# Two-layer decoder trunk on one core: smaller adding transfers in the MLP, and a later row scale in layer 1

## The chip, the cores and the metric

The kernel runs on one core of a Trainium2 chip. The metric is device time in microseconds. Three runs of the kernel before took 605.1, 606.25 and 607.38 us, a median of 606.25. The engines named below are TensorE (PE; PEld is its weight load), VectorE (DVE), ScalarE (ACT), GpSimd (POOL) and SyncE (SP), each with a queue of its own that is worked off in order.

## The reference

The input is one sequence of 256 rows with 1024 channels in 32-bit floats. Two layers follow each other, then a last RMSNorm.

```
h = x
for i in range(2):
    hn = rmsnorm(h, attn_norm[i])
    m  = diff_attention(hn, ...) if i == 0 else moba_attention(hn, ...)
    h  = h + m
    h  = h + square(relu(rmsnorm(h, mlp_norm[i]) @ w_ff1[i])) @ w_ff2[i]     # 1024 -> 4096 -> 1024
out = rmsnorm(h, final_norm)
```

Layer 0's mixer has 8 heads, each with two softmaxes whose difference weighs the values. Layer 1's has 16 heads of 64 channels with block choice, which at 256 rows and blocks of 256 comes to plain causal attention. Both project with one matrix w_in to q, k and v and then with w_out. Per layer that is 12 MB of w_in, 4 MB of w_out and 16 MB each of w_ff1 and w_ff2, all read from HBM.

## The kernel before, in words

**Splitting.** TensorE multiplies in a rounded form of 32-bit floats. To keep the accuracy, every operand is split into a high part (the rounded value) and a low part (what rounding left). A product is then three matmuls: high by high, high by low, low by high. All weights pass through this split on the chip.

**Blocks of weights.** Weights come in blocks of 1 MB (128 partitions x 2048 values). `load` (L148) issues a block's transfer on SP's queue into one of four `raw` buffers; the split writes `hi` and `lo` buffers, of which there are five each. A block's transfer waits until the split four blocks earlier has released its `raw` buffer; a split waits until TensorE has released a `hi` and `lo` buffer. `need` (L220) asks, wherever a matmul uses a block, for loads up to six blocks ahead and for splits up to three ahead.

**Three ways of splitting.** In the plain way (`split_part`, L194), ScalarE copies raw to the rounded high part (L195) and VectorE subtracts it from raw to get the low part (L196), in pieces of 1024 values, or in one piece of 2048 where a unit's `how` is the number RING (2048). The blocks of w_ff2 (`split_sums`, L165) also form sums and differences of their four quarters (L177, L179, L180), since the second product is done with seven matmuls in place of eight; their last step is a piece of 2048 (high by ScalarE, low by VectorE). The blocks of w_ff1 from column group j = 1 on are split "partly" (`split_partly`, L184). A block there has KC = 8 row groups of 256 values per partition. The first OWN = 3 groups are split in the plain way, in a piece of 768. For the other five, ScalarE writes the high part (L189) and then its negative into `lo` (L190), and a transfer that GpSimd issues (L191) reads the same weights from HBM a second time and adds them to `lo`.

```
k = slice(OWN, KC)
nc.scalar.activation(hi[:, k], raw[:, k], AF.Copy)
nc.scalar.activation(lo[:, k], hi[:, k].bitcast(F32), AF.Copy, scale=-1.0)
nc.gpsimd.dma_start(lo[:, k], units[u]["pieces"][0][1][:, k], accum_op=ALU.add)
split_part(raw[:, :OWN], hi[:, :OWN], lo[:, :OWN])
```

**The MLP.** `mlp` works through pairs of 256 hidden columns p = 0 to 15; blocks (j, a) of w_ff1 and w_ff2 belong to p = 2j + a. `f1` (L692) multiplies by a w_ff1 block: for each 128 columns it goes through the row groups kc = 0 to 7 with three matmuls each (L702, L703, L704; L704 uses `lo`). `hidden` (L708) makes the squared ReLU on ScalarE (L715, L716), its sums on VectorE (L720 to L722) and its split (gh, gl). `f2` (L730, matmuls at L744) multiplies by a w_ff2 block, two pairs behind; the products of pairs 13 and 14 come last (`product`), then pair 15 (`direct`, L754).

**The order.** Within the MLP and at the head of layer 1, no order is written out: a planner orders each engine's instructions from the program's order, the dependences and its own estimates of duration, with splits set back in priority (LATER). In the rest of the mixers TensorE's order is the program's. Layer 0's head has its whole order written out.

**The head of layer 1.** The mixer's first matmuls use the transposed, not yet scaled rows `xT`. The factor of each row, one over the root mean square, is computed by GpSimd (`root_r`, L326), spread over the partitions by two transposes on TensorE (`scale_r`, L384) and copied to `R` by ScalarE (L385, L386). `qk` (L388) accumulates q and k of a head pair into one bank `z` (L396 to L398), and `qk_out` (L402) multiplies `z` by `R` on VectorE (L405). In layer 1 the order of calls is: row groups 0 to 3 of head 0's q and k, the first half of v, `root_r`, `scale_r`, row groups 4 to 7 of head 0's q and k, the second half of v (L581 to L586).

Of the kernel before, what the change touches and what calls it, by code (L numbers as in the profile page):

```python
# [24 lines left out]
RING = 2048  # L25
# [2 lines left out]
WARM = 12  # L28
LATER = 150
SOONER = 100  # L30
OWN = 3


@with_exitstack
def kernel(
# [33 lines left out]
    def ptile(*a, **k):  # L69
        return phase["pool"].tile(*a, **k)  # L70
# [19 lines left out]
    units = []  # L90
# [6 lines left out]
    for i in range(2):  # L97
# [27 lines left out]
        def f1_unit(j, a):  # L125
            c = j * 512 + a * 256
            U[i, "f1", j, a] = unit([P, KC, 256], [((slice(None),), f1[:, :, c:c + 256])])
            if j:
                units[-1]["how"] = "partly"

        def f2_unit(j, a):
            U[i, "f2", j, a] = unit([P, 2, D], [
# [240 lines left out]
    def mixer(i, parts):  # L373
# [3 lines left out]
        def root_r():  # L377
            S["r"] = rsqrt(f"a{i}", mean_eps(f"a{i}", parts))

        def scale_r():  # L380
            r = S["r"]
            t_ps = ps("tp", f"rps{i}")
            for t in range(NT):
                nc.tensor.transpose(t_ps[:, t * P:(t + 1) * P], r[:, t:t + 1].to_broadcast([P, P]), ident)  # L384
            nc.scalar.activation(R[:, :T], t_ps[:, :T], AF.Copy, scale=-HD ** -0.5)  # L385
            nc.scalar.activation(R[:, T:], t_ps[:, :T], AF.Copy)  # L386
# [15 lines left out]
        def qk_out(h):  # L402
            o = ptile([P, 2 * T], F32, tag="qk", name=f"qk{i}_{h}", bufs=4)
            with tc.high_priority(offset=SOONER):
                nc.vector.tensor_tensor(o, S["z", h], R, op=ALU.mult)  # L405
            S["qk", h] = o[:, :T], o[:, T:]
# [155 lines left out]
        if i == 0:  # L562
            with tc.manual_schedule():
                parts = start()
                root_r()
                xt = xT[i, "a"]
                qk(0, 0, 0, 8, out=False)
                qk(0, 1, 0, 8, out=False)
                v(0, 0)
                split_until(3)  # L570
                lambda_sums()
                scale_r()
                qk_out(0)
                split_until(5)
                v(0, 1)
                lambda_out()
                load_gains()
            state["ahead"] = LOOK
        else:
            xt = xT[i, "a"]  # L580
            qk(0, 0, 0, 4); qk(0, 1, 0, 4)  # L581
            v(0, 0)
            root_r()
            scale_r()
            qk(0, 0, 4, 8); qk(0, 1, 4, 8)
            v(0, 1)  # L586


# [362 lines left out]
```

## Time and profile before

| What | Value |
|---|---|
| median of three runs | 606.25 us (605.1 to 607.38) |
| the profiled execution | 607.94 us, of which the span of instructions is 606.2 |
| TensorE busy | 577.5 us (95%) |
| VectorE busy | 460.8 us (76%) |
| ScalarE busy | 411.4 us (68%) |
| GpSimd busy | 104.1 us (17%) |
| bytes moved | 122.28 MB, of them 18.37 MB on GpSimd's queue |
| mean granted TensorE clock | 0.98 |

How to read it: all times are from one execution. "Busy" counts an engine's instructions, and "idle before" is the time an engine stood still ahead of an instruction, with the instruction that released it behind "<-". `lo<-in_w_ff_dram` on GpSimd's queue is the adding transfer; `raw<-in_w_ff_dram` on SP's is the plain load. Buffer numbers are left out of names. The granted clock is TensorE's share of full speed. A group's line gives its count, then busy time and mean ns of one instruction behind the first bar, and idle time behind the second.

### The profile page before, as it was taken

What the parts mean: (1) busy time and instruction counts of PE and PEld (TensorE: products, weight loads), DVE (VectorE), ACT (ScalarE), POOL (GpSimd) and SP (SyncE); (2) the same over time, 40 slices, a digit from 0 to 9 for tenths busy, and PEclk for the clock granted to TensorE, in tenths of its full rate; (3) what the DMA queues carried; (4) which work ended last, traced back from release to release, by engine and by line L of the source; (5) the groups of instructions that cost most, each with busy time, mean ns of one, the idle gap of its engine ahead of it and who ended that gap; (6) DMA issues with size and microseconds to landing.
All of it is one profiled execution on the core that took longest, in us unless ns stands there. A gap on an engine that the chain in (4) does not pass through costs nothing.

```text
span 606.2 us, 9768 instructions
## 1 busy us (share of the span) xinstructions
PE 577.5 (95%) x3784; PEld 516.0 (85%) x3784; DVE 460.8 (76%) x740; ACT 411.4 (68%) x640; POOL 104.1 (17%) x109
## 2 busy tenths in 40 slices
PE   7999998999899999997979999999999999999985
PEld 6899897799799898986769988878988999898964
DVE  3898487299889898977784664645997989888774
ACT  6876466388878778767464555646887787787543
POOL 6011001101110101100050760601011010110003
PEclk9999999999999999999899999999998999999978
DMA  9996633159999999974687535433699999999501
GB/s 299 288 318 209 189 103 128 68 115 270 263 286 231 271 255 252 317 178 127 199 244 203 179 140 148 139 131 50 169 265 279 249 272 222 275 250 273 148 0 69
DMA packets 103486, 122.28 MB, mean 202 GB/s; under 512 B 2544, under 2 KB 86288, under 8 KB 103440
## 3 DMA queue, kind: packets, MB, share of 16 engines
q1 hardware_dynamic: 84752, 103.03, 53.6%
q0 software_dynamic: 18528, 18.37, 20.0%
q8 instruction: 29, 0.48, 0.3%
q10 hardware_dynamic: 160, 0.27, 0.1%
q14 instruction: 17, 0.14, 0.1%
HBM read 120.60 MB, written 1.05 MB: 201 GB/s over the span
## 4 chain that ended last, share of the span: by engine, by line
PE 38%; DVE 24%; issue 14%; ACT 11%; DMA 9%; POOL 2%; SPq 0%; POOLq 0%; DVEq 0%; ACTq 0%
DVE lo L196 7%; DVE tlo L196 5%; PE z L396 5%; PE z L397 4%; PE m L744 4%; PE z L398 4%; DMA lo<-in_w_ff_dram 4%; DMA raw<-in_w_ff_dram 3%; DVE gl L196 3%; ACT hi L195 2%; DVE raw L180 2%; PE wo L552 2%; PE v L419 2%; PE v L417 2%; PE v L418 2%
## 5 line engine op out<-in xcount | busy, mean ns | idle before, releaser
L195 ACT ACTIVATE hi<-raw 128x1024 fp32r<-128x1024 f32 (+3 forms) x136 | 158.7, 1186 | 89.8 <-DVE raw L180 40.7
L196 DVE TENSOR_TENSOR lo<-raw,hi 128x1024 fp32r<-128x1024 f32 (+3 forms) x134 | 184.2, 1396 | 38.3 <-ACT hi L195 37.0
L191 POOL DMA_DIRECT2D lo<-in_w_ff_dram x28 | 42.2, 1508 | 285.6 <-ACT lo L190 224.5
L704 PE MATMUL f<-xT_(1, 'm')_4429,lo 128*128 128x256 f32 x256 | 72.3, 283 | 2.3 <-DMA lo<-in_w_ff_dram 2.3
L704 PE MATMUL f<-xT_(0, 'm')_1447,lo 128*128 128x256 f32 x256 | 71.4, 279 | 2.6 <-DMA lo<-in_w_ff_dram 2.6
L703 PE MATMUL f<-xT_(1, 'm')_4429,hi 128*128 128x256 f32 x256 | 72.1, 282 | 0.0
L702 PE MATMUL f<-xT_(1, 'm')_4429,hi 128*128 128x256 f32 x256 | 72.0, 282 | 0.0
L702 PE MATMUL f<-xT_(0, 'm')_1447,hi 128*128 128x256 f32 x256 | 71.5, 280 | 0.0
L703 PE MATMUL f<-xT_(0, 'm')_1447,hi 128*128 128x256 f32 x256 | 71.4, 280 | 0.0
L744 PE MATMUL m<-hi,gh 128*128 128x512 f32 x120 | 47.8, 401 | 4.6 <-ACT hi L195 4.6
L704 PEld LDWEIGHTS f<-xT_(1, 'm')_4429,lo 128*128 128x128 f32 x256 | 48.5, 190 | 2.7 <-DMA lo<-in_w_ff_dram 2.7
L744 PE MATMUL m<-lo,gh 128*128 128x512 f32 x120 | 49.0, 408 | 1.8 <-DVE lo L196 1.8
L704 PEld LDWEIGHTS f<-xT_(0, 'm')_1447,lo 128*128 128x128 f32 x256 | 47.9, 187 | 2.8 <-DMA lo<-in_w_ff_dram 2.8
L702 PEld LDWEIGHTS f<-xT_(1, 'm')_4429,hi 128*128 128x128 f32 x256 | 48.7, 191 | 0.7
L703 PEld LDWEIGHTS f<-xT_(1, 'm')_4429,hi 128*128 128x128 f32 x256 | 48.7, 190 | 0.6
L702 PEld LDWEIGHTS f<-xT_(0, 'm')_1447,hi 128*128 128x128 f32 x256 | 48.0, 188 | 0.9 <-ACT g L715 0.3
L703 PEld LDWEIGHTS f<-xT_(0, 'm')_1447,hi 128*128 128x128 f32 x256 | 48.0, 188 | 0.6
L744 PE MATMUL m<-hi,gl 128*128 128x512 f32 x120 | 48.4, 403 | 0.0
L195 ACT ACTIVATE gh<-g 128x1024 fp32r<-128x1024 f32 (+1 forms) x32 | 33.0, 1031 | 20.9 <-DVE g L722 20.6
L196 DVE TENSOR_TENSOR gl<-g,gh 128x1024 fp32r<-128x1024 f32 (+1 forms) x32 | 38.0, 1187 | 10.8 <-ACT gh L195 10.8
L189 ACT ACTIVATE hi<-raw 128x1280 fp32r<-128x1280 f32 x28 | 35.3, 1259 | 13.4 <-PE wo L554 13.4
L177 DVE TENSOR_TENSOR ts<-raw 128x1024 f32<-128x1024 f32 x30 | 36.5, 1218 | 6.4 <-DMA raw<-in_w_ff_dram 6.4
(232 smaller groups left out, 1475.4 us busy)
## 6 DMA issues: line engine op xcount, KB each, us to landing
raw<-in_w_ff_dram SPq DMA_DIRECT2D x64, 1024.0 KB, 6.6
lo<-in_w_ff_dram POOLq DMA_DIRECT2D x28, 640.0 KB, 10.2
raw<-in_w_in_dram SPq DMA_DIRECT2D x30, 512.0 KB, 6.8
raw<-in_w_in_dram SPq DMA_DIRECT2D x8, 1024.0 KB, 6.3
raw<-in_w_out_dram SPq DMA_DIRECT2D x8, 1024.0 KB, 5.1
xs<-in_x_dram SPq DMA_DIRECT2D x2, 512.0 KB, 3.8
raw<-in_w_in_dram SPq DMA_DIRECT2D x4, 256.0 KB, 7.0
fg<-in_final_norm_dram SPq DMA_DIRECT2D x1, 512.0 KB, 7.0
```

The costliest lines, as they stand in the source:

```text
L177: tt(ts, r4[:, 1:2].to_broadcast([P, 2, h]), r4[:, 0:4:3], op=sub)
L189: nc.scalar.activation(hi[:, k], raw[:, k], AF.Copy)
L191: nc.gpsimd.dma_start(lo[:, k], units[u]["pieces"][0][1][:, k], accum_op=ALU.add)
L195: nc.scalar.activation(h, r, AF.Copy)
L196: eng.tensor_tensor(l, r, h.bitcast(F32), op=ALU.subtract)
L396: mm(z, hi[:, s, kc], xh, start=s == 0 and kc == 0, stop=False, skip_group_check=True)
L397: mm(z, hi[:, s, kc], xl, start=False, stop=False, skip_group_check=True)
L398: mm(z, lo[:, s, kc], xh, start=False, stop=s == 1 and kc == KC - 1, skip_group_check=True)
L702: mm(z, hi[:, kc, c], xh, start=f % 2 == 0 and kc == 0, stop=False, skip_group_check=True)
L703: mm(z, hi[:, kc, c], xl, start=False, stop=False, skip_group_check=True)
L704: mm(z, lo[:, kc, c], xh, start=False, stop=f % 2 == 1 and kc == KC - 1, skip_group_check=True)
L744: mm(M[k], x[:, g], y, start=p == 0 and x is gh and y is hi, stop=p == LAST - 1 and x is gl, skip_group_check=True)
```

## The change

OWN becomes 5, so five of a partly split block's eight row groups are split in the plain way and the adding transfer covers three. The two blocks with j = 1 of each layer are no longer split partly but in the plain way, in one piece of 2048; they have no adding transfer. In layer 1, `scale_r` is called after row groups 4 to 7 of head 0's q and k, and `qk_out` for head 0 after it.

```diff
-OWN = 3
+OWN = 5
@@ f1_unit
             if j:
-                units[-1]["how"] = "partly"
+                units[-1]["how"] = "partly" if j > 1 else RING
@@ mixer, layer 1
             v(0, 0)
             root_r()
+            qk(0, 0, 4, 8); qk(0, 1, 4, 8, out=False)
             scale_r()
-            qk(0, 0, 4, 8); qk(0, 1, 4, 8)
+            qk_out(0)
             v(0, 1)
```

## The prediction

> **What bounds the kernel now.** First the page and the waits of TensorE (columns: us in total, times, longest). TensorE is busy 95% of the span, so only its stalls and its clock can be won.
>
> ```profile
> span 606.2 us, 9768 instructions
> PE 577.5 (95%) x3784; PEld 516.0 (85%) x3784; DVE 460.8 (76%) x740; ACT 411.4 (68%) x640; POOL 104.1 (17%) x109
> ...
> PE f L704 <- DMA lo<-in_w_ff_dram: 4.9, 2, 2.6
> PE m L744 <- ACT hi L195: 4.6, 2, 2.9
> PE rps L384 <- POOL rs_a L326: 3.3, 1, 3.3
> ...
> PE m L744 <- DVE lo L196: 1.8, 2, 0.9
> ```
>
> The change touches all four. The first sits early in each MLP: a matmul wants low parts that an adding transfer has not delivered. The second and fourth sit at the end of each MLP, on the split of the last block but one of w_ff2. The third sits at the head of layer 1.
>
> Then the busy time by stage (length, PE, PEld, DVE, ACT, POOL, granted clock, DMA share, GB/s). The first two rows are the MLPs of layers 0 and 1, from their first matmul to the end of that last split.
>
> ```profile
> 122.00:285.60 163.60, 157.30 (x1059) 143.71 (x1057) 142.77 (x176) 127.28 (x143) 19.70 (x14) 1.00 0.92 237
> 419.00:582.70 163.70, 158.91 (x1058) 145.31 (x1056) 142.74 (x175) 127.15 (x141) 19.54 (x13) 0.99 0.89 227
> ...
> 285.00:292.00 7.00, 6.31 (x15) 4.96 (x16) 7.00 (x8) 5.91 (x9) 0.00 (x0) 0.51 0.75 231
> ...
> 316.20:319.60 3.40, 3.36 (x18) 3.37 (x19) 0.00 (x0) 1.60 (x3) 0.00 (x0) 0.57 1.01 377
> ...
> 455.60:459.10 3.50, 3.14 (x14) 3.15 (x15) 2.91 (x4) 3.43 (x3) 0.00 (x0) 0.51 0.92 305
> ```
>
> The reader is to see three things. TensorE idles 6.3 us in the first MLP (163.60 less 157.30), VectorE 20.8. Behind a stall the granted clock falls to about half. And the two MLPs are equally long to 0.1 us although layer 1 has a stretch at half clock after its early stall (455.60) that layer 0 has not, some 1.7 us of TensorE time. What TensorE loses early in an MLP is therefore not seen at its end: the end is set by the chain of splits on VectorE and ScalarE. This decides how I cost the change.
>
> VectorE's own waits in layer 0's MLP, and its last turns:
>
> ```profile
> DVE gl L196 <- ACT gh L195: 5.4, 6, 1.2
> DVE g L720 <- ACT g L716: 4.6, 6, 1.0
> DVE lo L196 <- ACT hi L195: 4.3, 3, 2.0
> DVE ts L177 <- DMA raw<-in_w_ff_dram: 4.1, 2, 2.7
> ...
> 261.52 1.23 DVE L177 TENSOR_TENSOR ts<-raw 128x1024 f32<-128x1024 f32 x1 [2.73 <-DMA raw<-in_w_ff_dram]
> ...
> 273.34 2.29 DVE L196 TENSOR_TENSOR lo<-raw,hi 128x2048 fp32r<-128x2048 f32 x1 [1.98 <-ACT hi L195]
> ...
> 277.81 1.22 DVE L196 TENSOR_TENSOR gl<-g,gh 128x1024 fp32r<-128x1024 f32 x1 [1.19 <-ACT gh L195]
> ...
> 283.35 4.49 DVE L196 TENSOR_TENSOR lo<-raw,hi 128x2048 fp32r<-128x2048 f32 x2 [1.98 <-ACT hi L195]
> ```
>
> The three last turns (1.98, 1.19, 1.98: 5.2 us) are VectorE handing to ScalarE and waiting for the answer. They stay. The other waits on ScalarE (14.3 less 5.2: 9.1) and on transfers (4.1) are what can give way.
>
> **Part 1, the splits.** Durations of one instruction by shape (second number behind the bar, ns):
>
> ```profile
> L196 DVE TENSOR_TENSOR lo<-raw,hi 128x1024 fp32r<-128x1024 f32 x68 | 81.1, 1221 | 25.0 <-ACT hi L195 24.9
> L196 DVE TENSOR_TENSOR lo<-raw,hi 128x2048 fp32r<-128x2048 f32 x32 | 73.0, 2287 | 9.2 <-ACT hi L195 7.9
> ...
> L195 ACT ACTIVATE hi<-raw 128x2048 fp32r<-128x2048 f32 x32 | 61.1, 1915 | 41.0 <-DVE raw L180 40.7
> ...
> L190 ACT ACTIVATE lo<-hi 128x1280 fp32r<-128x1280 f32 x28 | 35.4, 1263 | 0.0
> ...
> L196 DVE TENSOR_TENSOR lo<-raw,hi 128x768 fp32r<-128x768 f32 x28 | 26.7, 952 | 0.8 <-ACT hi L195 0.8
> ...
> L195 ACT ACTIVATE hi<-raw 128x768 fp32r<-128x768 f32 x28 | 23.3, 833 | 0.0
> ```
>
> Now a partly split block of w_ff1 costs ScalarE two pieces of 1280 and one of 768 (1.26 + 1.26 + 0.83: 3.35 us) and VectorE one of 768 (0.95). After it, ScalarE has two of 768 and one of 1280 (2.92, so 0.43 less). VectorE has one of 1280, a shape without a row: between the rows of 1024 and 2048 a straight line gives 1.49, so 0.53 more; its ends are 1.22 and 2.29, and it stands near the first. The two blocks of j = 1 in each layer lose the transfer altogether: ScalarE 1.92 in place of 3.35 (1.43 less), VectorE 2.29 in place of 0.95 (1.34 more), and an issue on GpSimd goes. Per layer, with 12 blocks of the one kind and two of the other, VectorE gets 9.0 us more (6.4 and 2.7), ScalarE 8.0 us less (5.2 and 2.9). Adding transfers move 12 x 384 KB in place of 14 x 640 KB. Loads on SP's queue are as many as before; each starts when VectorE has freed its buffer.
>
> The early stall: its transfer was the third of the layer.
>
> ```profile
> 159.43 0.39 PE L704 MATMUL f<-xT_(0, 'm')_1447,lo 128*128 128x256 f32 x1 [2.59 <-DMA lo<-in_w_ff_dram]
> ...
> 146.59 12.79 DMA lo<-in_w_ff_dram
> ...
> DMA to landing us min/median/max: 7.3/10.2/12.8
> ```
>
> It will be the first, two fifths shorter, and TensorE asks for it two row groups later. Even if only a third of the 12.79 us goes, the 2.59 us of waiting are covered. So I expect no stall of TensorE there, and, by the equal lengths above, little of it in the total: the wait moves to the end of the MLP, where TensorE then stands earlier before the same split.
>
> What counts is when VectorE finishes. It has 9.0 us more to do and 20.8 us of idle time to do it in. The 4.1 us on transfers I take as gone, since the queue carries about half the added bytes. Of the 9.1 us on ScalarE each wait shrinks by what its pair of blocks brings: VectorE comes 0.53 later and ScalarE is 0.43 sooner, 0.96 against waits that are 1.2 at most. Nearly all would go; I take 6.5 and leave 2.6, because the waits for L716 also hang on TensorE's own matmuls. The MLP then ends 4.1 + 6.5 - 9.0 = 1.6 us sooner, 3.2 in two layers. From below: if no wait gave way it would end 9.0 later. From above: the 6.3 us that TensorE idles. The half clock at 285.00 I leave as it is, since TensorE still waits there.
>
> The Trainium skill, "DMA: Bandwidth & Descriptors", section "Anatomy of one DMA — SWDGE (gpsimd) path", gives a transfer that GpSimd issues as about 2.0 us plus bytes over 436e9. By it the cut of 256 KB would save an estimated 0.6 us, and it speaks against this change: mostly fixed cost stays. The rows above (7.3 to 12.8 us for one size) disagree with it here.
>
> **Part 2, layer 1's row scale.** What surrounds it now:
>
> ```profile
> 312.54 0.40 PE L419 MATMUL v<-hi,xT_(1, 'a')_3209 128*128 128x512 f32 x1
> 316.24 0.69 PE L384 MATMUL rps<-ident,rs_a 128*128 128x128 f32 x2 [3.30 <-POOL rs_a L326]
> 316.58 0.56 PE L396 MATMUL z<-xT_(1, 'a')_3209,hi 128*128 128x256 f32 x1
> ...
> 320.64 0.40 PE L417 MATMUL v<-hi,xT_(1, 'a')_3209 128*128 128x512 f32 x1
> ...
> 310.09 6.09 POOL L326 TENSOR_TENSOR rs_a<-mv_a,half 128x2 f32<-128x2 f32 x1 [4.26 <-DVE mv_a L321]
> ...
> 309.39 0.47 DVE L290 SCALAR_TENSOR_TENSOR xT_(1, 'a')_3209<-xtp_(1, 'a')_1_1_3234,gT,xT_(1, 'a')_3209 128x256 fp32r<-128x256 f32 x1
> ...
> 320.92 0.69 DVE L405 TENSOR_TENSOR qk<-z,R 128x512 f32<-128x512 f32 x1 [5.31 <-PE z L398]
> ...
> 320.41 0.28 PE L397 MATMUL z<-xT_(1, 'a')_3209,hi 128*128 128x256 f32 x1
> 320.53 0.28 PE L398 MATMUL z<-xT_(1, 'a')_3209,lo 128*128 128x256 f32 x1
> ...
> 334.89 1.51 PE s L436 x16
> ```
>
> GpSimd's root takes 6.09 us and TensorE stands before the two transposes of it. The change puts 24 matmuls of head 0 (two halves, four row groups, three products) ahead. Their operand is ready at 309.9, so they start at 312.77 and take 24 x 0.12 (320.41 to 320.53) = 2.88 us, to 315.65. The transposes start at 316.24 as now and v's second half at 316.58 in place of 320.64: 4.06 us sooner, of which 1.2 is the half clock at 316.20 that falls away because the hole is only 0.6 us. From below, if the clock falls all the same, 2.4 (half of 3.4 us lost); from above 4.65, if matmuls of v fill that hole too. I take 4.1. Queued behind the transposes are the two copies of the scale on ScalarE and head 0's scaling on VectorE, where VectorE waited 5.31 us anyway; that result is not asked for before the scores at 334.89. No transfer and no queue is passed.
>
> The Trainium skill, "TensorE: Matmul & The Clock Gate", Part 1, has the clock halved after an idle window of about 3.4 us that runs freely; by its rule a hole of 0.6 us leaves the clock alone, while the 3.30 us now could cost the half window that the trace shows.
>
> **Sum.** 4.1 + 3.2 = 7.3 us. The profiled execution took 607.94 us with 606.2 of span; it would take 600.6. It stands 1.7 above the median of the three runs, 606.25, which becomes 599.0.
>
> **Rivals.** (a) The splits only break even, the row scale alone pays: 606.25 - 4.1 = 602.2. For it: 9.0 us added to a stage whose end VectorE sets. Against: ScalarE gets 8.0 less.
>
> (b) The early stall goes through to the total after all. Then its 2.59 and 2.3 us (4.9 in all) and layer 1's 1.7 us of clock come on top of the row scale: 606.25 - 4.1 - 6.6 = 595.5. For it: transfers land sooner, so the last split may start sooner. Against: the equal lengths.
>
> (c) Slower: VectorE becomes the bound. Transfers come in time (4.1), but no wait on ScalarE shrinks because each is a turn like the last three; each MLP ends 9.0 - 4.1 = 4.9 us later, 9.8 in two, less 4.1: 612.0. It decides for the whole kernel from where less than about 7 of VectorE's 20.8 us give way. For it: 87% busy in the stage (142.77 of 163.60). Against: ScalarE is freed at the same places.
>
> (d) Transfers hardly land sooner, so the 4.1 us stay: each MLP ends 9.0 - 6.5 = 2.5 later, 5.0 in two, less 4.1: 607.1. By the skill's fit of a mostly fixed cost it would go this way; the rows so far bear it out little.
>
> (e) The change does not do what it says: the planner, which orders TensorE there, keeps the transposes ahead of head 0, and only the splits pay: 603.0.
>
> **Chances.** The forecast, 599.0 within about 597 and 601.5, gets 0.42; (a) 0.15, (b) 0.17, (c) 0.10, (d) 0.10, (e) 0.06. The planner may also order ScalarE and VectorE anew, which no row shows; it widens each case. I take 593 to 608: outside lie (c), a third of (b) and a few parts of (d), some 0.19. A measurement of this kernel can tell about 0.5% (3.0 us) from no change. Below 603.2 lie the forecast, (b), most of (a) and half of (e): 0.73. Within are the rest of (a) and (e) and most of (d): 0.16. Above is (c) and a tail: 0.11.
>
> **What would show it.** Right: no wait of L704 on the adding transfer early in either MLP; VectorE busy about 151.8 us in the stage and the stage one or two us shorter; TensorE still waiting at L744 on the last split, longer than 2.9 us; the wait of L384 under 1 us and the clock at 1.00 after it. Wrong: VectorE's waits on ScalarE as long as before with the stage longer (c); waits of L177 on transfers as now (d); the 24 matmuls behind the transposes (e); or the wait at L744 gone (b and better).

## The result and the profile after

The changed kernel takes 587.46 us (median of 4 executions, 585.89 to 588.11), the kernel before on the same chip 605.93 (605.1 to 607.38): a ratio of 0.9689, 95% interval 0.9661 to 0.9717. The gain is 18.5 us. Forecast was 599.0, within 593 to 608. In the table below, medians are over all executions, and the ratios leave out those that took over 1.5% longer than the fastest of the same kernel (five of the kernel before's, beside the first four experiments). Line numbers of the changed kernel lie one higher from L584 on (L705 is the old L704, L745 the old L744).

First the page of the profiled execution after (586.96 us), and TensorE's waits (total, times, longest):

```profile
span 585.2 us, 9725 instructions
...
PE 568.9 (97%) x3784; PEld 509.5 (87%) x3784; DVE 477.9 (82%) x740; ACT 396.1 (68%) x632; POOL 89.1 (15%) x105
...
q0 software_dynamic: 9760, 9.45, 10.8%
```

```profile
PE m L745 <- DVE lo L196: 3.6, 2, 1.8
PE o L518 <- DVE on L530: 2.5, 2, 1.5
```

Three of the four waits quoted before are gone: no wait of TensorE on an adding transfer is listed, none on GpSimd's root, none on the high part of the last split. The fourth, for the low part of that split, has grown from 1.8 to 3.6 us. Both waits for the last split together are down from 6.4 us (4.6 and 1.8) to 3.6.

Now the busy time in three stretches that follow each other: layer 0's MLP from its first matmul to the last one of `direct`, then layer 1's mixer, then layer 1's MLP (columns as in the prediction: length, busy time of PE, PEld, DVE, ACT, POOL, granted clock, DMA share, GB/s). The kernel before:

```profile
122.10:301.80 179.70, 173.31 (x1115) 156.51 (x1114) 155.75 (x191) 135.51 (x153) 19.60 (x14) 0.98 0.90 233
301.80:418.90 117.10, 113.54 (x780) 99.06 (x779) 67.14 (x146) 65.11 (x148) 39.95 (x42) 0.99 0.50 153
418.90:599.00 180.10, 175.23 (x1122) 158.56 (x1120) 154.07 (x191) 132.01 (x152) 23.65 (x18) 0.97 0.81 206
sum 476.90, PE 462.07 PEld 414.13 DVE 376.96 ACT 332.63 POOL 83.19; mean PE 154.02 PEld 138.04 DVE 125.65 ACT 110.88 POOL 27.73
```

The changed kernel:

```profile
121.10:293.60 172.50, 170.39 (x1116) 154.46 (x1115) 163.18 (x191) 128.27 (x150) 15.43 (x12) 1.00 0.78 222
293.60:405.60 112.00, 111.74 (x780) 97.61 (x779) 68.21 (x146) 64.75 (x148) 34.83 (x41) 1.00 0.50 153
405.60:578.00 172.40, 170.60 (x1121) 154.97 (x1121) 160.24 (x190) 124.56 (x147) 19.40 (x16) 1.00 0.67 190
sum 456.90, PE 452.73 PEld 407.03 DVE 391.63 ACT 317.59 POOL 69.66; mean PE 150.91 PEld 135.68 DVE 130.54 ACT 105.86 POOL 23.22
```

This is the account that the prediction should have kept. Length less TensorE's busy time is its idle time: 14.8 us before (476.90 - 462.07), 4.2 after. And its busy time itself falls by 9.3 us (462.07 to 452.73) for the same matmuls, because the granted clock no longer drops. The two add up to the 20.0 us by which the stretches are shorter. Another 1.0 us lies ahead of the first MLP and need not be the change's: the kernels below (e5 apart), whose edits all lie behind that point too, start it anywhere from 121.0 to 122.6 us. The profiled pair thus differs by 21.0 us, 2.5 more than the medians; the profiled execution of the kernel before (607.94) lies 2.0 above its median. VectorE does 14.7 us more work in these stretches and the kernel is faster: VectorE's work did not set the time.

### The profile page after: what moved, and what is told of

It is laid out like the page before. It is cut to its first block, busy times and chain, and to the rows that moved or that the text cites. A ratio compares the mean times of both kernels' runs of the same rounds, so it can differ in the third digit from the quotient of the medians.

```text
span 585.2 us, 9725 instructions
## 1 busy us (share of the span) xinstructions
PE 568.9 (97%) x3784; PEld 509.5 (87%) x3784; DVE 477.9 (82%) x740; ACT 396.1 (68%) x632; POOL 89.1 (15%) x105
## 4 chain that ended last, share of the span: by engine, by line
PE 75%; DVE 12%; ACT 6%; DMA 3%; issue 2%; POOL 1%; POOLq 0%; DVEq 0%; ACTq 0%
PE m L745 19%; PE f L704 8%; PE f L703 8%; PE f L705 8%; DVE lo L196 6%; PE z L396 4%; PE z L397 4%; PE z L398 4%; ACT hi L195 4%; PE wo L552 3%; PE wo L554 2%; PE wo L553 2%; PE v L417 2%; PE v L419 2%; PE v L418 2%
## 5 line engine op out<-in xcount | busy, mean ns | idle before, releaser
L196 DVE TENSOR_TENSOR lo<-raw,hi 128x1024 fp32r<-128x1024 f32 (+3 forms) x134 | 203.8, 1537 | 41.0 <-ACT hi L195 39.0
L703 PE MATMUL f<-xT_(0, 'm')_1444,hi 128*128 128x256 f32 x256 | 71.5, 280 | 0.3 <-ACT g L716 0.3
L704 PE MATMUL f<-xT_(1, 'm')_4420,hi 128*128 128x256 f32 x256 | 71.6, 280 | 0.0
L703 PE MATMUL f<-xT_(1, 'm')_4420,hi 128*128 128x256 f32 x256 | 71.5, 280 | 0.1
L704 PE MATMUL f<-xT_(0, 'm')_1444,hi 128*128 128x256 f32 x256 | 71.5, 280 | 0.0
L705 PE MATMUL f<-xT_(1, 'm')_4420,lo 128*128 128x256 f32 x256 | 71.3, 279 | 0.0
L705 PE MATMUL f<-xT_(0, 'm')_1444,lo 128*128 128x256 f32 x256 | 71.3, 279 | 0.0
L745 PE MATMUL m<-lo,gh 128*128 128x512 f32 x120 | 47.7, 398 | 3.6 <-DVE lo L196 3.6
L703 PEld LDWEIGHTS f<-xT_(0, 'm')_1444,hi 128*128 128x128 f32 x256 | 48.0, 188 | 1.3 <-ACT g L716 0.7
L703 PEld LDWEIGHTS f<-xT_(1, 'm')_4420,hi 128*128 128x128 f32 x256 | 48.0, 188 | 1.1 <-ACT g L716 0.5
L704 PEld LDWEIGHTS f<-xT_(0, 'm')_1444,hi 128*128 128x128 f32 x256 | 48.0, 188 | 0.6
L704 PEld LDWEIGHTS f<-xT_(1, 'm')_4420,hi 128*128 128x128 f32 x256 | 48.0, 188 | 0.6
L705 PEld LDWEIGHTS f<-xT_(1, 'm')_4420,lo 128*128 128x128 f32 x256 | 47.9, 187 | 0.0
L705 PEld LDWEIGHTS f<-xT_(0, 'm')_1444,lo 128*128 128x128 f32 x256 | 47.9, 187 | 0.0
L745 PE MATMUL m<-hi,gh 128*128 128x512 f32 x120 | 47.6, 396 | 0.0
L745 PE MATMUL m<-hi,gl 128*128 128x512 f32 x120 | 47.2, 393 | 0.0
L177 DVE TENSOR_TENSOR ts<-raw 128x1024 f32<-128x1024 f32 x30 | 36.5, 1218 | 5.2 <-DMA raw<-in_w_ff_dram 5.2
L196 DVE TENSOR_TENSOR gl<-g,gh 128x1024 fp32r<-128x1024 f32 (+1 forms) x32 | 37.7, 1184 | 0.0
L396 PE MATMUL z<-xT_0a,hi 128*128 128x256 f32 x128 | 36.7, 287 | 0.3 <-ACT hi L195 0.3
```

Source lines behind the costliest of these rows:

```text
L177: tt(ts, r4[:, 1:2].to_broadcast([P, 2, h]), r4[:, 0:4:3], op=sub)
L196: eng.tensor_tensor(l, r, h.bitcast(F32), op=ALU.subtract)
L396: mm(z, hi[:, s, kc], xh, start=s == 0 and kc == 0, stop=False, skip_group_check=True)
L703: mm(z, hi[:, kc, c], xh, start=f % 2 == 0 and kc == 0, stop=False, skip_group_check=True)
L704: mm(z, hi[:, kc, c], xl, start=False, stop=False, skip_group_check=True)
L705: mm(z, lo[:, kc, c], xh, start=False, stop=f % 2 == 1 and kc == KC - 1, skip_group_check=True)
```

## The experiments

The table puts all runs side by side: in each stretch TensorE's idle time (length less busy), and how long the granted clock stood at half, from the profiled execution's clock record. Half clock costs about half its length (before: 20.4 us at half, 9.3 us more busy time). Medians were taken beside the kernel before on the same chip (606.64 us for the first four rows of runs, 606.47 for the next four, 605.1 for the next four, 605.77 for the last two). Single executions of the kernel before lay between 598 and 610 us, those of the changed kernel between 585.9 and 588.1. Idle time and half clock are those of one execution each, which need not be a typical one: that of e3 is the fastest of its ten, 596.65 us.

| Kernel | median us | ratio to before, 95% | layer 0 MLP idle / half | layer 1 mixer | layer 1 MLP |
|---|---|---|---|---|---|
| before | 605.93 | 1 | 6.4 / 6.8 | 3.6 / 3.4 | 4.9 / 10.2 |
| changed | 587.46 | 0.9661 to 0.9717 | 2.1 / 0 | 0.3 / 0 | 1.8 / 0 |
| e1_own5 | 591.29 | 0.9731 to 0.9900 | 2.8 / 3.4 | 0.3 / 0 | 3.1 / 0 |
| e2_plain_first | 591.38 | 0.9731 to 0.9892 | 1.3 / 0 | 3.5 / 3.4 | 1.3 / 0 |
| e3_scale | 601.94 | 0.9925 to 1.0018 | 4.5 / 3.4 | 0.3 / 0 | 5.4 / 3.4 |
| e4_short | 596.34 | 0.9811 to 0.9971 | 3.2 / 3.4 | 3.6 / 3.4 | 1.8 / 0 |
| e6_third_plain | 605.25 | 0.9959 to 1.0018 | 6.5 / 0 | 3.5 / 3.4 | 6.7 / 3.4 |
| e7_tail | 593.47 | 0.9703 to 0.9803 | 2.8 / 0 | 1.0 / 0 | 3.9 / 3.4 |
| e8_ahead | 600.86 | 0.9854 to 0.9939 | 3.4 / 0 | 4.4 / 6.8 | 2.5 / 0 |
| e9_after_ahead | 585.92 | 0.9611 to 0.9682 | 0.0 / 0 | 1.1 / 0 | 0.4 / 0 |
| e10_old_turns | 591.03 | 0.9712 to 0.9796 | 2.0 / 0 | 0.6 / 0 | 2.0 / 3.4 |
| e13_new_turns | 599.64 | 0.9848 to 0.9944 | 5.5 / 6.8 | 0.3 / 0 | 5.6 / 6.8 |
| e12_no_scale | 587.14 | 0.9647 to 0.9729 | 1.7 / 0 | 0.3 / 0 | 1.7 / 0 |
| e5_bytes_back | 659.79 | 1.0778 to 1.0930 | 1.8 / 3.4 | 0.3 / 0 | 2.0 / 3.4 |
| e14_gap | 600.11 | 0.9878 to 0.9948 | 5.8 / 10.2 | 0.3 / 0 | 5.1 / 6.8 |
| e15_bytes_tied | 588.33 | 0.9664 to 0.9748 | 2.8 / 0 | 0.3 / 0 | 2.8 / 3.4 |

### The parts of the change, each alone

**e1_own5**: the kernel before with the size alone.

```diff
-OWN = 3
+OWN = 5
```

> Only the split sizes: five of eight row groups split in the plain way in all 28 partly split blocks, j = 1 too; layer 1's head as before. Measured so far: the whole change takes 18.5 us off, of which its trace puts about 7.3 and 7.7 us in the two MLPs and 4.8 us at layer 1's head. Theory D (bytes: with shorter adding transfers the loads land sooner, the last split of each MLP comes sooner, and the clock stays up): the added bytes fall from 8960 to 5376 KB a layer here, to 4608 in the whole change, so most of the MLP gain comes from this part: 9 to 14 us faster. Theory V (the ledger of the prediction: VectorE's added 0.53 us a block against ScalarE's 0.43 us less decides): 2 to 6 us faster. Theory P (the planner's new order of the engines in the whole change did it): not to be told from the sizes; near 0 if the order here stays like that of before.

**e2_plain_first**: the kernel before with the j = 1 blocks alone.

```diff
-                units[-1]["how"] = "partly"
+                units[-1]["how"] = "partly" if j > 1 else RING
```

> Only the two blocks of j = 1 in each layer split in the plain way; the others keep three groups plain and five by the adding transfer. Theory D: the early wait of TensorE for the adding transfer goes, but the transfers later in the MLP are as long as before, so the end of the MLP stays where it was, as in the prediction's reading that early loss is not seen at the end: 0 to 3 us faster. Theory V: VectorE gets 2.7 us more a layer: 0 to 5 us slower. Theory P (order): as much as 10 us faster.

**e3_scale**: the kernel before with the later row scale alone.

```diff
             root_r()
+            qk(0, 0, 4, 8); qk(0, 1, 4, 8, out=False)
             scale_r()
-            qk(0, 0, 4, 8); qk(0, 1, 4, 8)
+            qk_out(0)
```

> Only the row scale of layer 1 behind head 0's q and k. All theories: 4 to 5 us faster, the wait of L384 under 1 us and no half clock at that place; the MLPs as before, with their waits and their half clock.

**e4_short**: the kernel before with a shorter adding transfer and no split moved. Two of its five row groups are left out, so that their low parts stay the negative of the high part: this work is missing from the result.

```diff
-        nc.gpsimd.dma_start(lo[:, k], units[u]["pieces"][0][1][:, k], accum_op=ALU.add)
+        kk = slice(OWN + 2, KC)
+        nc.gpsimd.dma_start(lo[:, kk], units[u]["pieces"][0][1][:, kk], accum_op=ALU.add)
```

> The kernel before with its instructions on ScalarE and VectorE unchanged (three groups plain, five prepared for the transfer), but the adding transfer covers only three of those five groups; the low parts of the other two groups stay at the negative of the high part, so this leaves part of the work out. Bytes added fall by two fifths, the engines' work stays. Theory D: the MLP gain of the short transfer comes alone, without VectorE's added work: 9 to 15 us faster, at least as much as with five groups split plainly. Theory V (ScalarE's saved time is what counts): within 3 us of before.

Measured: 591.29, 591.38, 601.94 and 596.34 us. Either edit of the splits alone takes the median 15 us below that of the kernel before beside it (6 to 16 us by the intervals), and both with the move 18.5: they take from the same idle time, and their gains don't add. In e2 VectorE has more to do and the remaining transfers move as many bytes as before, yet both MLPs are 8 us shorter. In e4 VectorE and ScalarE have the same work as before, no wait of TensorE on an adding transfer is left, and the MLPs are 4.8 and 7.5 us shorter. No split's work moved there, so the shorter transfers did this, with whatever order the planner made of them. TensorE's waits in e2:

```profile
PE rps L384 <- POOL rs_a L326: 3.2, 1, 3.2
...
PE m L744 <- DVE lo L196: 1.3, 2, 0.7
PE m L744 <- ACT hi L195: 1.3, 2, 0.7
```

The early stall is gone, and instead of growing by it, as the prediction held, the waits at the end shrank from 6.4 us (4.6 and 1.8) to 2.6, with no half clock behind them. The move alone (e3) is not told apart from no change over its executions, though its profiled one has lost the wait at the transposes.

### Is it the early stall, or the order at the end?

The planner orders VectorE, ScalarE and TensorE anew for every edit, so the four runs above differ in more than their edit. The next two are meant to change little else, though the order shifts with them too.

**e6_third_plain**: the kernel before; only the block whose transfer TensorE waits for early is split in the plain way.

```diff
-                units[-1]["how"] = "partly"
+                units[-1]["how"] = RING if (j, a) == (2, 0) else "partly"
```

> The kernel before, with one edit: of the blocks of w_ff1 only (2, 0) of each layer, whose adding transfer TensorE waits for early (2.59 us in layer 0, 2.3 us and a half clock of about 1.7 us in layer 1), is split in the plain way. One adding transfer of 640 KB fewer per layer, 1.34 us more on VectorE. Theory L (the prediction's: what TensorE loses early is not seen at the end): 604 to 608 us, the end waits of TensorE grow by what it gains early. Theory S (the early stall goes through to the end of the MLP): at least 2.59 + 2.3 + 1.7 = 6.6 us less, 599 us or below; 591 if the waits and the half clock at the end go as well, as in the kernel where both blocks of j = 1 were plain (591.4).

Measured: 605.25 us, no change. That is the time of Theory L, but not its picture: the waits for the last split did not grow (6.2 us in place of 6.4). Theory S is wrong in this form too: TensorE passes the old place and waits for the adding transfers behind it and, late in each MLP, for the step on ScalarE that makes the hidden rows (L715). The waits of e6:

```profile
PE m L744 <- ACT hi L195: 5.8, 2, 2.9
PE f L704 <- DMA lo<-in_w_ff_dram: 3.5, 4, 1.3
PE f L702 <- ACT g L715: 3.4, 2, 1.8
```

Two waits on the adding transfer have become four shorter ones. With two transfers fewer, both early ones (e2), nothing of it is left.

**e7_tail**: the kernel before; a copy of nothing (one element per partition, times zero, added) makes the sums of block (7, 0) of w_ff2 wait for the low part of block (7, 1) of w_ff1.

```diff
         r4 = raw.rearrange("p f (n c) -> p (f n) c", n=2)
+        if u in (U[0, "f2", 7, 0], U[1, "f2", 7, 0]):
+            nc.vector.scalar_tensor_tensor(raw[:, 0, 0:1], units[u - 2]["lo"][:, 0, 0:1].bitcast(F32), 0.0,
+                                           raw[:, 0, 0:1], op0=ALU.mult, op1=ALU.add)
```

> The kernel before, with one order changed: an instruction of one element per partition makes VectorE take the sums of the last but one block of w_ff2, (7, 0), only after the low parts of the two blocks ahead of it, (6, 0) of w_ff2 and (7, 1) of w_ff1. Before, VectorE stands 2.73 us at these sums for their load while those low parts queue behind. Theory O (what was gained at the end is this order, which the planner changed with the transfers): the last split ends 2 to 3 us sooner in each layer and the half clock there goes: 597 to 601 us. Theory S (early stall plus end wait that follows from it): within 2 us of before, 604 to 608 us, since the two splits that end the MLP still hang on the same load.

Measured: 593.47 us, 13 us less than the kernel before beside it, and more than Theory O expected. No transfer and no split was changed. VectorE in layer 0, at the place where the prediction's rows show it standing 2.73 us before L177 (line numbers are 3 higher here: L180 is the old L177, L199 the old L196, and L178 is the copy of nothing):

```profile
259.03 2.29 DVE L199 TENSOR_TENSOR lo<-raw,hi 128x2048 fp32r<-128x2048 f32 x1
...
263.35 0.95 DVE L199 TENSOR_TENSOR lo<-raw,hi 128x768 fp32r<-128x768 f32 x1
264.34 0.16 DVE L178 SCALAR_TENSOR_TENSOR raw<-lo,raw 128x1 f32<-128x1 f32 x1
264.53 1.23 DVE L180 TENSOR_TENSOR ts<-raw 128x1024 f32<-128x1024 f32 x1
```

The low parts go first and the sums start without a wait. The two early stalls are still there (5.1 us), but TensorE's idle time in layer 0's MLP falls from 6.4 to 2.8 us, and the half clock at its end is gone. So an order of a few VectorE instructions, which no line of the change names, can be worth most of what the whole change is worth. Not all of it lies at the end of the MLPs: 3.8 us of the profiled gain are in layer 1's mixer, where VectorE's order has changed too (see "Layer 1's head"). And it is not the order that the changed kernel has: there the sums of (7, 0) still stand ahead, but VectorE waits 1.03 us for their load in place of 2.73.

### The last turns

The prediction held that VectorE's three last turns with ScalarE (1.98, 1.19, 1.98) stay. In the changed kernel the second and third are gone, because the difference of L180 now stands before `gl`:

```profile
270.23 2.29 DVE L196 TENSOR_TENSOR lo<-raw,hi 128x2048 fp32r<-128x2048 f32 x1 [1.98 <-ACT hi L195]
...
273.90 0.68 DVE L180 TENSOR_TENSOR raw<-raw 128x512 f32<-128x512 f32 x1
274.50 1.22 DVE L196 TENSOR_TENSOR tlo<-ts,thi 128x1024 fp32r<-128x1024 f32 x1
275.64 1.22 DVE L196 TENSOR_TENSOR gl<-g,gh 128x1024 fp32r<-128x1024 f32 x1
276.98 4.49 DVE L196 TENSOR_TENSOR lo<-raw,hi 128x2048 fp32r<-128x2048 f32 x2
```

**e10_old_turns** puts the old turns into the changed kernel, **e13_new_turns** the new ones into the kernel before, each with a gate of one element.

```diff
# e10_old_turns, on the changed kernel, in split_sums (state["gl"] is set to gl in hidden)
...
+        if u in (U[0, "f2", 7, 0], U[1, "f2", 7, 0]):
+            nc.vector.scalar_tensor_tensor(r4[:, 2, 0:1], state["gl"][:, 0, 0:1].bitcast(F32), 0.0,
+                                           r4[:, 2, 0:1], op0=ALU.mult, op1=ALU.add)
         tt(r4[:, 2], r4[:, 2], r4[:, 1], op=sub)
# e13_new_turns, on the kernel before, in f2 at p == LAST - 3: low() writes pair 14's gl, r94 is block (7, 0) of w_ff2
...
+                nc.vector.scalar_tensor_tensor(g[:, 0, 0:1], r94[:, 2, 0:1], 0.0, g[:, 0, 0:1],
+                                               op0=ALU.mult, op1=ALU.add)
+                low()
```

> The changed kernel with one order put back as it was before: an instruction of one element per partition makes VectorE write the low part of pair 14's hidden rows (gl) before the last difference of block (7, 0) of w_ff2 (L180), so that ScalarE's high part of that block is asked for late again. Everything else is the changed kernel's, transfers included. Theory O (a good part of the gain is the order of VectorE's last turns, which came along with the change): the last split ends about 2.0 us later in each layer, TensorE's wait there grows from 2.3 to over 4 us: 591.5 us, and up to 598 if the clock falls behind the longer wait. Theory B (the gain is in the bytes that are no longer moved): within 1.5 us of the changed kernel, 586 to 589 us.

> The kernel before with the opposite order change alone: the low part of pair 14's hidden rows (gl) is written after the last difference of block (7, 0) of w_ff2 (L180), as in the changed kernel; splits, transfers and the rest of the order as before. Theory O: the wait of 1.19 us for gh and one turn of 1.98 us fall away, the last split ends about 3 us sooner in each layer, the wait for its high part (3.30 us) is gone and with it the half clock (3.4 us): 593 us; 600 us if the clock falls all the same. Theory B: 604 to 608 us.

Measured: e10 591.03, e13 599.64. The medians look like Theory O, the stretches don't. In e10 layer 0's MLP is as long as in the changed kernel (172.5), TensorE waits as long (3.9 us for the high part in place of 3.6 for the low one), and layer 1's MLP is 1.5 us longer, with a half clock of 3.4 us. What else its profiled execution is longer by, 1.2 us ahead of the first MLP, 0.6 in the mixer and 1.1 after the last matmul, was not followed. In e13 both MLPs are within 0.9 us of before, and its gain lies in layer 1's mixer (112.5 us in place of 117.1). So the new turns alone don't give the gain, and the old ones alone take little of it away (3.6 us of the median). Neither run isolates them, though, since TensorE's order changed with them: in e13 the last low part starts 1.7 us sooner (281.65 in place of 283.35), but TensorE asks for it one matmul after its wait for the high part, in the kernel before five matmuls after it, and in layer 0 both wait 3.4 to 3.8 us for the two; in e10 the low part starts 3.1 us later, and TensorE asks for it later too.

### TensorE's hole, and the clock behind it

**e8_ahead** and **e9_after_ahead**: the kernel before and the changed one with all matmuls of pair 13 ahead of the first of pair 14, so that 4.2 us of work stand in the hole.

```diff
-            if p < LAST:
-                f2(p - 2, SEVEN)
+            f2(p - 2, SEVEN)
...
-            for p in range(LAST - 2, LAST):
-                f2(p, (k,))
+            f2(LAST - 1, (k,))
```

> The kernel before, with TensorE's order at the end of the MLP changed: all 21 matmuls of pair 13 come before the first of pair 14, so 18 of them (18 x 0.2325 = 4.2 us) stand in the hole where TensorE waited 3.30 and 1.28 us for the split of block (7, 0). Splits and transfers are as before. If the hole cost its own length alone: about 4 us less per layer, 598 us. If the half clock that follows it (6.8 us long, worth 3.4) is caused by the hole: about 6.5 us less per layer, 593 us, and no half clock at the end of either MLP. If the end is set by VectorE and ScalarE whatever TensorE does meanwhile: within 2 us of before. The early stall stays in all cases.

> The changed kernel with the same order of TensorE at the end of the MLP (pair 13's 21 matmuls ahead of pair 14). Its waits there are 2.32 and 2.13 us. If they are plain holes: 4 us less, about 583.5 us. If the adds behind the products, now at a pace of three matmuls each, come late on VectorE: the wait moves there, 586 to 589 us.

Measured: 600.86 and 585.92 us. In e8 the MLPs shrink by 5.3 and 7.1 us and no half clock is left in them. That is more than the hole alone (about 4 expected) and about the hole with its clock (6.5). But 2.5 us come back in the mixer, 1.7 of them since the clock stands at half there for 6.8 us in place of 3.4, and 2.7 after the last matmul, where the adds and the last norm now come behind TensorE. In e9 the MLPs have hardly any idle time left:

```profile
121.30:291.50 170.20, 170.20 (x1116) 154.75 (x1114) 161.30 (x187) 129.22 (x148) 15.43 (x12) 1.00 0.79 221
291.50:405.00 113.50, 112.43 (x781) 97.47 (x780) 69.84 (x150) 64.81 (x148) 35.85 (x41) 1.00 0.52 156
405.00:575.80 170.80, 170.37 (x1122) 155.14 (x1120) 159.53 (x188) 123.29 (x144) 18.32 (x15) 1.00 0.68 191
```

Of the 4 us won there, 1.5 return in the mixer and 1.3 at the end. Its interval (0.9611 to 0.9682) overlaps that of the changed kernel: it is the fastest kernel measured, but not told apart.

What a hole does to the clock is seen best inside one execution, e6. The last split is awaited equally long in both layers (timeline of TensorE), and the windows behind the two waits differ:

```profile
283.63 0.73 PE L744 MATMUL m<-hi,gh 128*128 128x512 f32 x2 [2.90 <-ACT hi L195]
...
579.03 1.22 PE L744 MATMUL m<-hi,gh 128*128 128x512 f32 x2 [2.90 <-ACT hi L195]
```

```profile
283.70:290.50 6.80, 6.37 (x27) 4.85 (x28) 6.80 (x6) 6.80 (x9) 0.00 (x0) 1.00 0.47 162
579.00:582.40 3.40, 3.37 (x8) 2.70 (x9) 3.40 (x2) 3.34 (x4) 0.00 (x0) 0.51 0.00 0
```

After 2.90 us of waiting the clock stays at 1.00 once and falls to 0.51 once; in the kernel before it stayed down for 6.8 us. The traces also show why. All half-clock stretches of one execution start on one grid with a step of 3.413 us: in the kernel before at 285.02, 315.74, 455.68 and 581.98 us, which are 9, 50 and 87 steps behind the first. Here are the two steps of e6's grid that hold the wait in layer 0, and the one that holds it in layer 1:

```profile
278.66:282.07 3.41, 2.07 (x15) 1.58 (x13) 2.97 (x4) 1.25 (x2) 0.00 (x0) 1.00 0.53 205
282.07:285.49 3.42, 1.86 (x7) 1.23 (x7) 1.88 (x1) 3.42 (x3) 0.00 (x0) 1.00 0.00 0
...
575.62:579.03 3.41, 0.51 (x4) 0.07 (x2) 1.44 (x3) 1.97 (x2) 0.00 (x0) 1.00 0.00 0
```

In layer 0 the grid cuts the wait, and TensorE idles 1.34 us in one step and 1.56 in the next; in layer 1 all 2.90 us fall into one step, and the clock falls at its end. Over the sixteen profiled executions, the clock fell 46 times. In the step before, TensorE had idled at least 1.70 us each time; behind the steps at full clock that did not end so, it had idled at most 1.89. So about half a step of idle time within one step decides, worked out from the profile's modelled ends of matmuls, and where the grid lies differs from execution to execution.

The Trainium skill, "TensorE: Matmul & The Clock Gate", Part 1, has a free-running activity window of about 3.4 us, with the half clock after an idle window. The trace agrees in the length (every half-clock stretch of the MLPs is 3.4 or 6.8 us long). Taken at its word, that needs a hole of about 3.4 us, and there the measurement differs: the clock also falls behind a hole of 1.82 us (e15, next).

### Do the bytes count?

**e5_bytes_back** and **e15_bytes_tied**: the changed kernel with a second adding transfer of 256 KB per block into a scratch tile, which VectorE zeroes once at the start. In e5 nothing ties it to its block, in e15 one element copied from the block's high part does.

```diff
...
         nc.gpsimd.dma_start(lo[:, k], units[u]["pieces"][0][1][:, k], accum_op=ALU.add)
+        nc.gpsimd.tensor_copy(scratch[:, 0, 0:1], hi[:, OWN, 0:1].bitcast(F32))     # e15 only
+        nc.gpsimd.dma_start(scratch, units[u]["pieces"][0][1][:, 0:2], accum_op=ALU.add)
```

> The changed kernel with the removed bytes put back: behind each adding transfer a second one, of 256 KB from the same block, adds into a scratch tile that nothing reads (the zeroing of the tile at the start is the one instruction more). The order on TensorE, VectorE and ScalarE is the changed kernel's. Theory B (fewer bytes let the loads land sooner, and this is the gain): the load of block (7, 0) takes over 10 us again in place of 8.0, VectorE waits 2 to 3 us longer at its sums, and the kernel takes 592 to 598 us. Theory O: within 2 us of the changed kernel, 586 to 589 us.

> The changed kernel with the removed bytes put back inside the MLPs: ahead of each adding transfer of 384 KB a second one of 256 KB from the same block adds into a scratch tile that nothing reads; one element of the tile is copied from the block's high part first, so that it can't run earlier. TensorE, VectorE and ScalarE keep the changed kernel's order (VectorE zeroes the tile once at the start). The transfers of j = 1 stay away. Theory B (fewer bytes let loads and adding transfers land sooner and the gain hangs on it): TensorE waits again for low parts and, longer than 2.3 us, for the last split: 592 us or more. Theory H (the later transfers had room; what counts is that no transfer runs early, the order, and that TensorE's holes stay too short for the clock to fall): TensorE's holes in each MLP within 1 us of the changed kernel's 2.0 and 1.8 us, 587 to 590 us.

e5 took 659.79 us and answers another question. All its extra transfers were ordered into layer 0's mixer, each waiting for the one before, and GpSimd's roots and biases stood behind them: the first MLP starts at 191.9 us in place of 121.1. GpSimd's rows there:

```profile
58.23 1.20 POOL L194 DMA_DIRECT2D scratch<-in_w_ff_dram  x1 [6.35 <-DMA scratch<-in_w_ff_dram]
66.34 1.20 POOL L194 DMA_DIRECT2D scratch<-in_w_ff_dram  x1 [6.90 <-DMA scratch<-in_w_ff_dram]
```

e15 has them at their place, each issued just ahead of its block's adding transfer, which now lands after 9.6 us (median) in place of 7.9: 588.33 us. Its MLPs:

```profile
121.30:294.60 173.30, 170.53 (x1116) 154.71 (x1115) 163.35 (x191) 128.44 (x150) 47.03 (x36) 1.00 0.91 239
...
406.60:581.50 174.90, 172.15 (x1121) 155.98 (x1120) 160.38 (x190) 124.64 (x147) 51.45 (x40) 0.99 0.79 205
```

TensorE idles 2.8 us in each in place of 2.1 and 1.8, and the second has one half clock, behind this wait (timeline of TensorE, then the window; below them the same two of the changed kernel; L749 and L200 are the old L744 and L196):

```profile
565.52 0.50 PE L749 MATMUL m<-lo,gh 128*128 128x512 f32 x1 [1.82 <-DVE lo L200]
...
566.60:570.00 3.40, 3.40 (x10) 2.62 (x9) 2.93 (x4) 0.63 (x2) 0.00 (x0) 0.51 0.00 0
```

```profile
563.64 0.50 PE L745 MATMUL m<-lo,gh 128*128 128x512 f32 x1 [1.74 <-DVE lo L196]
...
564.70:568.10 3.40, 3.40 (x16) 2.78 (x15) 3.30 (x5) 0.66 (x2) 0.00 (x0) 1.00 0.00 0
```

So the 256 KB less per block are worth up to about 1 us of idle time per MLP. The half clock in layer 1 comes on top in this execution: one step of its grid holds 1.83 us of idle time, where no step of the changed kernel's there holds more than 1.10. Theory H holds: the later transfers had room.

### Layer 1's head

**e12_no_scale**: the changed kernel with the calls of layer 1's head as before.

```diff
             root_r()
-            qk(0, 0, 4, 8); qk(0, 1, 4, 8, out=False)
             scale_r()
-            qk_out(0)
+            qk(0, 0, 4, 8); qk(0, 1, 4, 8)
```

> The changed kernel with the row scale of layer 1 back in its old place. By the prediction's term (4.1 us) and by the 4.9 us that the head of layer 1 gave in the kernel with the move alone: 591.5 to 592.3 us. If GpSimd's root already starts sooner with the changed end of the MLP, as in the kernel with OWN = 5 alone, where TensorE had no wait over 0.6 us at the transposes: 587 to 589 us.

Measured: 587.14 us, and the mixer takes 112.3 us, as with the move (112.0). The third part of the change is worth nothing measurable beside the other two. What differs from before is the root itself, GpSimd's instruction that computes the rows' factor. GpSimd's row, and VectorE at the same time, in the changed kernel (timelines):

```profile
300.99 1.56 POOL L326 TENSOR_TENSOR rs_a<-mv_a,half 128x2 f32<-128x2 f32 x1 [2.08 <-DVE mv_a L321]
...
300.75 1.21 DVE L196 TENSOR_TENSOR lo<-raw,hi 128x1024 fp32r<-128x1024 f32 x1
301.89 0.47 DVE L290 SCALAR_TENSOR_TENSOR xT_(1, 'a')_3203<-xtp_(1, 'a')_1_0_3227,gT,xT_(1, 'a')_3203 128x256 fp32r<-128x256 f32 x1
```

In the kernel before the root took 6.09 us, and VectorE ran five subtractions without a gap:

```profile
309.85 5.76 DVE L196 TENSOR_TENSOR lo<-raw,hi 128x1024 fp32r<-128x1024 f32 x5
```

In e2 it took 4.96 us under four, in e7 2.69 under two, in layer 0, where it starts ahead of VectorE's, 0.73. One run doesn't fit: in e3 it took 1.55 us though three subtractions ran in a row over it, without a gap.

**e14_gap**: the kernel before; behind each of these subtractions VectorE copies one element.

```diff
...
                         split_piece(u0, c, piece)
+                        if 48 <= u0 < 56:
+                            lo = units[u0]["lo"].rearrange(letters(units[u0]["shape"]))
+                            nc.vector.tensor_copy(gap, lo[:, c:c + 1].bitcast(F32))
```

> The kernel before, with a copy of one element per partition behind each low-part subtraction of layer 1's first eight weight blocks on VectorE, so that the five subtractions that ran back to back while GpSimd computed the row factor (6.09 us) now have short gaps between them. TensorE's order is as before. Theory K (GpSimd's root stands until VectorE's chain of subtractions has a gap; the head of layer 1 gained by this and not by the order of calls): the root takes about 1.6 us, TensorE's wait of 3.3 us at the transposes and the half clock behind it (3.4 us long, worth 1.7) go: about 5 us less, 600 us. Rival (the 6.09 us are the root's own, or what else GpSimd has to do there): 604 to 608 us, root still 5 us or longer.

Measured: 600.11 us, as Theory K has it; the mixer takes 112.3 us in place of 117.1. GpSimd and VectorE (L331 is the old L326, L198 the old L196, L222 the copy):

```profile
311.27 1.62 POOL L331 TENSOR_TENSOR rs_a<-mv_a,half 128x2 f32<-128x2 f32 x1 [5.38 <-DVE gap L222]
...
311.10 1.21 DVE L198 TENSOR_TENSOR lo<-raw,hi 128x1024 fp32r<-128x1024 f32 x1
312.23 0.14 DVE L222 COPY gap<-lo 128x1 f32<-128x1 f32 x1
312.30 1.21 DVE L198 TENSOR_TENSOR lo<-raw,hi 128x1024 fp32r<-128x1024 f32 x1
```

The root ends at 312.89, 0.58 us after the end of the subtraction that it started under (312.31); before, at 316.18, 0.57 after the end of the fifth (315.61). The Trainium skill, "SBUF — State Buffer", section "SBUF: two separate sides", says that VectorE with two operands in SBUF and GpSimd exclude each other at a shared port for whole instructions. The trace agrees that the root waits, and adds that in all these runs but e3 it waited for the last subtraction of a chain and not for the first.

## Why the prediction was wrong, point by point

**Right.** The 1280 piece on VectorE takes 1489 ns (interpolated: 1.49), and the totals moved as costed: VectorE 460.8 to 477.9 us (8.6 per layer, forecast 9.0), ScalarE 411.4 to 396.1 (7.7 less, forecast 8.0). The early waits on the adding transfer are gone; the wait at L384 is gone and the clock behind it stays at 1.00. VectorE's waits for `gh` (5.4 us) and for L716 (4.6 us) are gone from layer 0's MLP up to the last split.

**Wrong, the step that decided:** "What TensorE loses early in an MLP is therefore not seen at its end: the end is set by the chain of splits on VectorE and ScalarE." It rested on the equal lengths of the two MLPs. The prediction's own rows show that these came about by chance: layer 1's TensorE is 1.6 us longer busy, for its half clock, and idles 1.5 us less. Over the whole MLP they are equal by two different sums as well: 179.70 us hold 6.4 idle and 6.8 at half clock, 180.10 hold 4.9 and 10.2. In every MLP here without a half clock, TensorE's busy time is 170.2 to 171.1 us, whatever VectorE does (170.39 and 170.60 after, 170.20 and 170.37 in e9); the rest of the length is holes. And early stalls are seen at the end: in e7 they stay and the last wait shrinks, and layer 0's MLP idles 2.8 us, of which 2.0 are the early stall. The term that followed from the step, 1.6 us per layer, came from VectorE's ledger; the MLPs measured 7.2 and 7.7 us less, beyond even the bound from above (6.3). The ledger itself was off as well: in layer 0, up to the last split, VectorE's work rose by 6.2 us (142.77 to 148.98) and not by 9.0, and its idle time fell by 11.5 (20.8 to 9.3) and not by 10.6. Rival (b), 595.5, had the mechanism nearest, and e6 shows why it can't be had by itself: with one early transfer gone, TensorE stalled at the next ones; with both gone (e2), it didn't.

**Wrong: "The half clock at 285.00 I leave as it is, since TensorE still waits there."** TensorE does still wait (1.8 us in each layer), but the clock stays at 1.00. The clock as a whole is worth 9.3 us in the profiled pair: 2.9 in layer 0's MLP, 4.6 in layer 1's and 1.8 in the mixer. The sum had 1.2, for the mixer. Part of this is luck: in layer 0 1.73 us of the wait fall into one step of the grid, where 1.70 us or more made the clock fall elsewhere, and one of the four executions of the changed kernel (588.11 us) has a mean clock of 0.994 in place of 0.998.

**Wrong: the last turns "stay", and TensorE waits longer than 2.9 us at L744.** Two of the three turns went, and the waits there are 1.8 us each. The order of the planner was named as something "which no row shows"; it is more than a widening of the range: e7 moves 13 us with it alone. What exactly shortened the last wait in the changed kernel stays open. Bytes on GpSimd's queue are up to 1 us of it per MLP (e15), and the last turns alone don't do it (e10, e13). That a third cause, the load of block (7, 0), now lands sooner relative to VectorE's queue is argued, not shown.

**Part 2: size about right, cause wrong.** Forecast 4.1 us; the mixer is 5.1 shorter. That the number came near is luck: the 6.09 us of the root were taken as its own duration. They were VectorE's chain (e14), and with another order of VectorE the wait falls away without the move (e12) or the gain comes without it (e14, e7, e13). What the move is worth beside a root of 6 us, no run shows: in every run with the move the root was shorter.

**The rule against the change.** The fit that the prediction cites from the Trainium skill ("DMA: Bandwidth & Descriptors", section "Anatomy of one DMA — SWDGE (gpsimd) path") put the saving of 256 KB at an estimated 0.6 us a transfer. The trace doesn't agree: with as many transfers as before (e4) the median landing fell by 1.4 us, 10.2 to 8.8, and in the changed kernel to 7.9. In time, the shorter early transfers end the early stalls (e4), while the later ones had room (e15).

## What to carry to other kernels

Where one engine is busy 95% of the span, keep its own account: length = busy at full clock + holes + half the time at half clock; everything that another engine's ledger predicts has to show up as a hole there. Behind a hole of 2 to 3 us the clock may fall, which cost another 1.7 us here (3.4 us at half) or 3.4 (6.8 us), so price both outcomes. With a planner, every edit also reorders: before crediting an edit, change one order alone with a gate of one element, and see what that is worth.

## What the runs showed of the hardware that I had not expected

GpSimd's instruction on two values per partition takes 0.73 us ahead of VectorE's subtractions, and 1.6, 2.7, 5.0 or 6.1 us started under one, two, four or five of them in a row (with the exception of e3: 1.6 us under three); one VectorE instruction of 0.14 us with a single SBUF operand lets it through (e14).

The clock fell behind holes of 1.8 to 3.3 us in some places and not in others, in the same execution; what decides is how much of the hole falls into one step of a grid of 3.413 us (at least 1.70 us in all 46 cases). This goes with the spread of the kernel before against that of the changed kernel: fewer holes go with a shorter and steadier time. The time lost to the clock in an execution is its span times one less the mean granted clock. Over the 42 executions of the kernel before that ran beside the experiments it goes from 4.2 to 14.6 us. Taken off, it leaves 592 to 599 us of the 598 to 610, so the clock makes up most of the spread, but not all.
